# Gate projections of blocks two to four by seven half-size products, with prepared weight combinations, gating in token halves, and a new stage order

## The chip, the cores and the metric

The kernel runs on one core of one Trainium2 chip. The metric is the device time in microseconds (us) of one execution. A core has a matrix engine (TensorE, PE, with a separate row for its weight loads, PEld), three engines for element-wise work (VectorE or DVE, ScalarE or ACT, GpSimd or POOL), and a queue engine (SyncE, SP) that issues nearly all DMAs of this kernel. Each engine works through its own list of instructions in order.

## The reference

One decoder layer on x of 2048 tokens by 1024 columns, in float32:

```python
n = _rms_norm(h, attn_norm_w[l])
proj = jnp.einsum('bsd,dc->bsc', n, w_in[l])
(gq, gk, gv, gg, ga, gb, rq, rk, rv, rg) = jnp.split(proj, split_idx, axis=-1)
o_gdn = _gated_deltanet(gq, gk, gv, gg, ga, gb, ...)
o_ret = _retention(rq, rk, rv, rg)
mix = jnp.concatenate([o_gdn, o_ret], axis=-1)
h = h + jnp.einsum('bsm,md->bsd', mix, w_out[l])
n2 = _rms_norm(h, mlp_norm_w[l])
h = h + _conv_glu_mlp(n2, w_up[l], mlp_conv_w[l], w_down[l])
return _rms_norm(h, final_norm_w)
```

Both head groups have 4 heads of 128 columns. The delta-rule group (gdn) carries a 128x128 state per head through the sequence; retention does the same with a fixed decay. The gates gg and rg, 512 columns each, are 1024 of the projection's columns. They enter only at the end of the mixer, where the normalized output of each head is multiplied by silu of its gate.

## The kernel before

Every float32 matmul is made of three passes with operands split in two parts, a high part (ACT copies it into the reduced type) and a low part (DVE subtracts the high part from the source): high by high, high by low, low by high. `mm3` (lines 108 to 113) issues the three passes; their matmuls are recorded as L111, L112, L113. A token-major projection, `tokmajor` (lines 375 to 387), issues the same three passes as L383, L384, L385.

The kernel has three stages. The mixers work through the sequence in four blocks of 512 tokens. MLP up (`mlp_up`) and MLP down (`mlp_down`) then each work on all 2048 tokens.

Large products are done by a scheme with seven half-size products in place of eight (the Strassen-Winograd form): both operands are cut into four quarters, sums and differences of quarters are formed, seven products are computed, and their results are added. Before the change the output projection of each block (items W1 to W7), MLP up and MLP down are computed so. The input projections, the gates among them, are plain.

A mixer block consists of named items: `pro` (load x, norms), `k0`, `q0`, `kq`, `v0` (retention projections, token-major), `a0` to `a3` (gdn projections of one head, channel-major, tile name chm), `b0`, `b1` (`gdn_base`: triangular inverse of 32x32 blocks, a long serial series on POOL, L603 and L605), `g0`, `g1` (`gdn_lvls` and four steps `gdn_rec` of the recurrence, then `gdn_fin`, for a pair of heads), `h0` to `h3` (retention heads), `p0`, `p1` (the gate projections, `gates`, 512 columns each: half gdn, half retention), `G0`, `G1` (`gated`: factor times gate, 32 PE transposes a block, tiles mix and mxt), `W1` to `W7` (output products), `N` (norm and transposes for the MLP, nps).

A recurrence step is a series over engines: PE (ks, L679), DVE (L682), PE (wps, L690), DVE (L694), PE (sps, L698), DVE (state, L700). `gdn_fin` makes the norm factor of all four steps with a power function on POOL (L716), and `gated` multiplies with it.

The string `ORDER` (lines 41 to 46) lists the items of all four blocks in one sequence, the first character being the block. The program is traced in this order; a scheduler then fixes the order of each engine's instructions before the run, with the traced order as priority, so that later items may fill time in which earlier ones wait for their inputs. Buffer counts per tile name (`BUFS`, `NWV` and others) limit how far ahead this goes.

Weights: `load_chunk` (lines 262 to 286) loads a projection's weights. In block one it reads them raw, splits them on ACT and DVE (L279, L280) and writes the split form to DRAM (wd); later blocks read it back (L273, tiles wc, 512 KB each). The gate weights are 16 such tiles a block. The weights of the output products are made by `load_v` (lines 154 to 193): in block one it loads quarters of the weight matrix for each product (wvr), forms the combination on POOL (L177), splits it (L197, L198), and writes it to DRAM (L192); later blocks read it back (L162, tiles wv, 5 buffers). `load_v` also serves MLP down (tiles vr, vt, v), where it forms every product's combinations anew.

`with tc.issue_after(ins)` queues what it encloses behind `ins` on the same engine's list: issue order only, no wait for the end of `ins`. Before the change the first weights and the x of MLP up are placed so behind one x load of block four's first output product (`FENCE`, lines 1079 to 1084).

Of the kernel before, what the change touches and what calls it, by code (L numbers as in the profile page):

```python
# [8 lines left out]
F32 = mybir.dt.float32  # L9
# [17 lines left out]
NWV = 5  # L27
FX = 1
NU = 4
NPB = 8  # L30
# [10 lines left out]
ORDER = ("0pro 0k0 0v0 0dec 0a0 0q0 0a1 0a2 0h0 0b0 0h1 0a3 0b1 0g0 0kq 0g1 0h2 0p1 1pro 0p0 1k0 0G0 0h3 "  # L41
# [37 lines left out]
def hybrid_block(ctx, tc, x, xT, w_kq, w_v, w_g, w_rk, w_r0, w_r, w_o, w_u, w_d, cols, rows, fnr, masks, rot, out):  # L79
# [28 lines left out]
    def mm3(ps, pairs, first=True, chk=False):  # L108
        n = len(pairs)
        for i, (ah, al, bh, bl) in enumerate(pairs):  # L110
# [11 lines left out]
           for q in range(2) for i in range(1, 8)}  # L122

    items = mixers(ctx, tc, base, o, marks, drp, mm3, gamma, mhalf, n1w, n2w, gcw, gv127, epsr, gnw, n2d, hd,
                   x, xT, w_kq, w_v, w_g, w_rk, w_r0, w_r, w_o, rows, masks, rot)
# [9 lines left out]
    for i, it in enumerate(seq):  # L135
# [3 lines left out]
        if it[0] is not None:  # L139
            it[2](loaded.pop(i))  # L140
# [7 lines left out]
    mlp_down(tc, marks, mm3, sfa, mhalf, hd, aud, w_d, fnr, out)  # L148
# [5 lines left out]
def load_v(tc, pool, w, i, k, tags, kept=None, drp=None):  # L154
# [5 lines left out]
    if kept is not None and (i, k) in kept:  # L160
        v = mk("v", F32R)
        nc.sync.dma_start(v.bitcast(F32), kept[i, k])  # L162
        return v
# [25 lines left out]
    v = split_v(nc, mk("v", F32R), src)  # L189
    if kept is not None:  # L190
        kept[i, k] = drp.tile([P, 2, TB], F32, name=f"wo{i}_{k}", tag=f"wo{i}_{k}", bufs=1)
        nc.sync.dma_start(kept[i, k], v.bitcast(F32))  # L192
    return v
# [9 lines left out]
def mixers(ctx, tc, base, base_used, marks, drp, mm3, gamma, mhalf, n1w, n2w, gcw, gv127, epsr, gnw, n2d, hd,  # L203
# [52 lines left out]


    WQ = 264
    cache = {}
    uses = {}  # L260

    def load_chunk(key, src):
# [1025 lines left out]
```

## Time and profile before

| what | value |
|---|---|
| median of 3 runs | 2495.26 us (2492.26 to 2498.91) |
| span of the profiled execution | 2495.3 us |
| granted TensorE clock, mean | 0.993 |
| PE busy | 2414.8 us (97%), 12476 matmuls |
| DVE, ACT, POOL busy | 1621.8, 1001.3, 579.7 us |
| DMA | 609.64 MB, 244 GB/s mean |

The profiled execution's own time is its span, from the first to the last instruction. In the groups of instructions a row gives line, engine, operation, output and input tiles, shape and count, then busy time, the mean of one in ns, and the idle time of the engine just before. Matmuls are pipelined, so that the means of neighbouring matmuls overlap. In the stretches the columns after the length are the busy time of PE, PEld, DVE, ACT and POOL, the granted clock, the share of time the DMA engines were busy, and GB/s.

### The profile page before, as it was taken

To read this page: it belongs to the slowest core of one execution; us is meant where nothing else is said; L and a number is where in the kernel's file an instruction comes from. 1 tells how busy PE (TensorE), PEld (TensorE's weight loads), DVE (VectorE), ACT (ScalarE), POOL (GpSimd) and SP (SyncE) were. 2 spreads that over 40 slices of the span, in tenths; PEclk is the share of its full clock that TensorE was granted. 3 is DMA by queue.
4 is the path that set the end of the run, shared out by engine and by line. 5 is a ranking of instruction groups with operands and counts; after the bars stand their busy time and mean duration, and the time that the engine had idled before them with its cause. 6 is when DMAs were issued, how large, how long until landed. Compare 5 with 4: busy or idle time off the path is not lost.

```text
span 2495.3 us, 35737 instructions
## 1 busy us (share of the span) xinstructions
PE 2414.8 (97%) x12476; PEld 2022.8 (81%) x12476; DVE 1621.8 (65%) x3199; ACT 1001.3 (40%) x2152; POOL 579.7 (23%) x891
## 2 busy tenths in 40 slices
PE   8999899999999999998899999999999999999998
PEld 7877787887888878887688888888888888888877
DVE  5845776435652673536889888896565567555795
ACT  6544544434342552425464344442222225332332
POOL 1354146521046205140011000010000001521180
PEclk9999999999999999999999999999999999999999
DMA  8756498863865646643889887867676868764794
GB/s 326 253 183 243 166 328 301 283 224 117 300 214 162 213 178 228 232 168 136 335 338 347 303 300 292 297 257 277 225 261 234 288 235 279 222 218 142 238 295 135
DMA packets 285748, 609.64 MB, mean 244 GB/s; under 512 B 40896, under 2 KB 120960, under 8 KB 285568
## 3 DMA queue, kind: packets, MB, share of 16 engines
q1 hardware_dynamic: 268992, 593.06, 67.7%
q10 hardware_dynamic: 16576, 14.30, 1.8%
q8 instruction: 98, 1.61, 0.3%
q14 instruction: 82, 0.67, 0.1%
HBM read 410.56 MB, written 196.71 MB: 243 GB/s over the span
## 4 chain that ended last, share of the span: by engine, by line
PE 76%; POOL 8%; DMA 6%; DVE 5%; issue 3%; ACT 2%; SPq 0%; ACTq 0%; POOLq 0%; DVEq 0%
PE p L111 10%; PE p L112 10%; PE p L113 10%; PE d L113 5%; PE d L111 4%; PE d L112 4%; PE tok L383 4%; PE tok L385 4%; PE tok L384 4%; POOL pers L605 3%; POOL pers L603 3%; PE chm L111 2%; PE chm L112 2%; PE chm L113 2%; PE wo L111 1%
## 5 line engine op out<-in xcount | busy, mean ns | idle before, releaser
L112 PE MATMUL p<-x,wu 128*128 128x512 f32 x1176 | 458.6, 390 | 4.2 <-DVE x L929 4.2
L111 PE MATMUL p<-x,wu 128*128 128x512 f32 x1176 | 454.4, 391 | 5.2 <-ACT x L928 3.8
L113 PE MATMUL p<-x,wu 128*128 128x512 f32 x1176 | 450.9, 389 | 0.0
L383 PE MATMUL tok<-wc,n 128*128 128x512 f32 (+2 forms) x768 | 275.4, 363 | 10.1 <-ACT n L371 8.4
L384 PE MATMUL tok<-wc,n 128*128 128x512 f32 (+2 forms) x768 | 276.7, 361 | 0.0
L385 PE MATMUL tok<-wc,n 128*128 128x512 f32 (+2 forms) x768 | 275.2, 362 | 0.0
L111 PEld LDWEIGHTS p<-x,wu 128*128 128x128 f32 x1176 | 220.8, 188 | 54.7 <-ACT x L928 6.5
L112 PEld LDWEIGHTS p<-x,wu 128*128 128x128 f32 x1176 | 220.8, 188 | 51.7 <-DVE x L929 6.4
L113 PEld LDWEIGHTS p<-x,wu 128*128 128x128 f32 x1176 | 220.9, 188 | 45.6
L1049 DVE SCALAR_TENSOR_TENSOR acc<-uc,base,acc 128x1022 f32<-128x1022 f32 (+1 forms) x176 | 221.1, 1278 | 39.8 <-ACT acc L1046 38.3
L1007 DVE TENSOR_TENSOR uc<-p,uc 128x512 f32<-128x512 f32 x224 | 153.0, 685 | 134.7 <-PE p L113 134.1
L177 POOL TENSOR_TENSOR vt<-vr 128x512 f32<-128x512 f32 x44 | 71.7, 1635 | 613.0 <-DMA vr<-in_w_d 439.3
L111 PE MATMUL d<-v,uu 128*128 128x512 f32 x448 | 174.4, 389 | 0.0
L113 PE MATMUL d<-v,uu 128*128 128x512 f32 x448 | 174.4, 389 | 0.0
L112 PE MATMUL d<-v,uu 128*128 128x512 f32 x448 | 174.4, 389 | 0.0
L383 PEld LDWEIGHTS tok<-wc,n 128*128 128x128 f32 x768 | 146.5, 191 | 29.7 <-ACT n L371 8.4
L384 PEld LDWEIGHTS tok<-wc,n 128*128 128x128 f32 x768 | 146.3, 191 | 19.3
L385 PEld LDWEIGHTS tok<-wc,n 128*128 128x128 f32 x768 | 145.1, 190 | 19.3
L111 PE MATMUL chm<-n,wc 128*128 128x512 f32 x384 | 152.3, 397 | 0.0
L113 PE MATMUL chm<-n,wc 128*128 128x512 f32 x384 | 152.3, 397 | 0.0
L112 PE MATMUL chm<-n,wc 128*128 128x512 f32 x384 | 152.1, 396 | 0.0
L1054 POOL COPY base<-uc 128x2 f32<-128x2 f32 x44 | 40.9, 929 | 451.1 <-DVE uc L1007 451.1
(250 smaller groups left out, 4857.6 us busy)
## 6 DMA issues: line engine op xcount, KB each, us to landing
wu<-wu SPq DMA_DIRECT2D x308, 512.0 KB, 6.0
wc<-wd SPq DMA_DIRECT2D x166, 512.0 KB, 5.1
wv<-wo SPq DMA_DIRECT2D x84, 512.0 KB, 5.4
wd<-wc SPq DMA_DIRECT2D x60, 512.0 KB, 4.2
ur<-au SPq DMA_DIRECT2D x56, 512.0 KB, 5.4
wur<-in_w_u SPq DMA_DIRECT2D x44, 512.0 KB, 5.9
au<-st SPq DMA_DIRECT2D x88, 256.0 KB, 4.8
vr<-in_w_d SPq DMA_DIRECT2D x44, 512.0 KB, 6.1
```

The lines of the kernel that those rows point to most:

```text
L111: PE.matmul(ps, ah, bh, start=(first and i == 0), stop=False, skip_group_check=chk)
L112: PE.matmul(ps, ah, bl, start=False, stop=False, skip_group_check=chk)
L113: PE.matmul(ps, al, bh, start=False, stop=(i == n - 1), skip_group_check=chk)
L177: POOL.tensor_tensor(tt[:, j], a, b_, op=ALU.subtract)
L383: PE.matmul(ps, ah, wh, start=(k == 0), stop=False)
L384: PE.matmul(ps, ah, wl, start=False, stop=False)
L385: PE.matmul(ps, al_, wh, start=False, stop=(k == KT - 1))
L603: POOL.tensor_tensor(tm[:, :, :n], Nb[:, j:j + 1, j + 1:].to_broadcast([P, 8, n]), X[:, :, j:j + 1].to_broadcast([P, 8, n]), op=ALU.mult)
L605: POOL.tensor_tensor(X[:, :, j + 1:], X[:, :, j + 1:], tm[:, :, :n], op=ALU.add)
L1007: add = lambda o, ps, a: DVE.tensor_tensor(o, ps, a, op=ALU.add)
L1049: DVE.scalar_tensor_tensor(acc[:, t:], u[:, :T2 - t], w, acc[:, t:], op0=ALU.mult, op1=ALU.add)
L1054: POOL.tensor_copy(mhalo[:, ci], u[:, T2 - 2:])
```

## The change

Gates: block one keeps the two plain projections (items p0, p1). In blocks two to four they are replaced by seven products B1 to B7 over tokens (2 x 256), input columns (2 x 512) and gate columns (2 x 512, array w_i). The item `s` (`combs`) loads the block's x once more and forms four combinations; `product` splits them when it first needs them, and adds the results up. Gates are now held as four tiles of 128 tokens by 1024 columns (C, Cb).

Weight combinations: the items Q0 to Q3 (output weights) and P0 to P3 (gate weights), one per K-tile, load four quarters once, form all combinations with four subtractions on POOL, split all seven and write them to DRAM (`prep_v`). Every product then reads its tiles back, in block one too (`kept_v`), through the same 5 buffers wv. These loads are `chained`: each is queued behind the previous one on SP, and behind the last load of the projection before. The gate weights' split form is no longer written by `load_chunk`.

Gating: `gated` works on tokens 0 to 255 (items G0a, G1a) and 256 to 511 (G0b, G1b) apart; the recurrence steps are single items (r00 to r13), and `gdn_fin` is called after every second step for half the tokens.

Others: MLP up's first weights and each quarter of its x are placed behind loads of block four's last output product (`FW`, `F0` to `F3`). In MLP down the combination made for product 6 is written to DRAM (t2d), and product 4 is made from it with one subtraction in place of three. Buffer counts and `ORDER` are new.

```diff
-FX = 1
-NU = 4
-NPB = 8
+FW = -3
+F0 = -4
+F1 = -3
+F2 = -2
+F3 = -1
+NU = 5
+NPB = 7
...
-BUFS = {"n1": 8, "ykq": 5, "kv": 4, "NT": 5, "AT": 6, "o": 2, "n2s": 11, "xk": 2, "og": 1, "co": 6, "Cw": 4,
-        "wx": 1, "wsq": 3, "wvr": 3, "wvt": 8, "ca": 8, "mix": 6, "D": 8, "rk": 5, "rq": 4, "rv": 8, "Ar": 1,
-        "Nb": 6, "rot": 1, "rrow": 7}
+BUFS = {"n1": 8, "ykq": 5, "kv": 5, "NT": 8, "AT": 8, "o": 2, "n2s": 11, "xk": 2, "og": 9, "co": 6, 
+        "Cw": 6, "wx": 1, "wsq": 1, "pr": 4, "pt": 7, "pv": 2, "ca": 4, "D": 8, "rk": 3, "rq": 9, "rv": 5, 
+        "Ar": 2, "xs": 6, "sx": 2, "Cb": 14, "Nb": 1, "rot": 1, "rrow": 1}
...
+ORDER = ("0pro 0k0 0dec 0v0 0a0 0q0 0a1 0a2 0h0 0h1 0a3 0b0 0Q0 0L0 0r00 0b1 0L1 0r01 0r02 0r03 0r10 0r11 "
+         "0r12 0r13 0kq 0Q1 0h3 0p1 1pro 0p0 0Q3 0h2 1k0 0Q2 0G1a 0G1b 0G0a 1v0 1dec 0W1 0G0b 0W2 0P3 1a0 1q0 "
+         "1a1 0W6 0W7 1h1 0W5 0W3 0W4 1a2 1h0 0P0 1b0 0N 1kq 1L0 1r00 0P2 1s 1r01 0P1 1a3 1B1 1B2 1B6 1r02 "
+         "1r03 1h2 1B7 1G0a 1b1 1L1 1r10 1r11 2pro 1B5 1B3 1h3 1B4 2k0 1r12 1r13 2v0 1G1a 1G1b 1G0b 2dec 1W1 "
+         "1W2 2a0 1W6 2a1 2a3 2b0 2a2 1W7 2b1 1W5 2q0 2L0 1W4 2h1 2r00 1W3 2r01 2h0 2r02 2r03 2L1 2r10 3pro "
+         "2r11 2s 2B1 2B2 2B6 2r12 2G0a 2r13 2B7 1N 2kq 2B5 2h2 2h3 2B4 2G0b 2B3 3k0 3dec 2G1a 2G1b 3a1 3a0 "
+         "2W1 3b0 2W2 2W6 2W7 3v0 3a2 3q0 3h1 3h0 2W5 3a3 3B1 3L0 3r00 3b1 3r01 3kq 3r02 3s 3B2 3L1 2W3 3h2 "
+         "3G0a 3r10 2W4 3r03 3B6 3r11 3r12 3r13 3B7 3B5 3B4 3B3 2N 3h3 3G1a 3W1 3G1b 3W2 3G0b 3W6 3W7 3W5 3W3 "
+         "3W4 3N")
...
+def chained(tc, marks, dst, src):
+    with tc.issue_after(marks["sp"].ins) if "sp" in marks else nullcontext():
+        marks["sp"] = tc.nc.sync.dma_start(dst, src)
+    marks.setdefault("vl", []).append(marks["sp"])
+def prep_v(tc, pool, marks, w, k, nm, kept, drp, caps):
...
+    for d, a, b_ in ((t1, q[1], q[0]), (t3, q[3], q[1]), (t2, q[3], t1), (t4, q[2], t2)):
+        POOL.tensor_tensor(d, a, b_, op=ALU.subtract)
+    for i, src in ((1, q[0]), (2, q[2]), (3, q[3]), (5, t1), (7, t3), (6, t2), (4, t4)):
+        v = split_v(nc, unit(pool, "pv", [P, 2, TB], F32R, bufs=caps[2]), src)
+        kept[i, k] = drp.tile([P, 2, TB], F32, name=f"{nm}{i}_{k}", tag=f"{nm}{i}_{k}", bufs=1)
+        nc.sync.dma_start(kept[i, k], v.bitcast(F32))
...
-                if keep:
+                if keep and key[0] != "g":
...
+        def combs(_):
...
+                for i, d, op, a, b_ in ((5, a22, ALU.add, a21, a22), (7, a21, ALU.subtract, a11, a21),
+                                        (6, a11, ALU.subtract, a22, a11), (3, a12, ALU.subtract, a12, a11)):
+                    DVE.tensor_tensor(d, a, b_, op=op)
+                    st["sr"][i, j] = d
...
+        def product(i):
+            def f(_):
+                ws = [kept_v(wic, i, k) for k in range(4)]
+                if i in (5, 6, 7, 3) and (i, 0) not in st["sx"]:
+                    for j in range(2):
+                        x_ = st["sx"][i, j] = al("sx", [P, 2, 2, TB // 2], F32R)
+                        split_v(nc, x_, st["sr"][i, j])
...
+                if i in (1, 5):
+                    st["ps"] = [bank("pi") for m in range(2)]
+                pss = st["ps"] if i in (1, 2, 3, 5) else [bank("pi") for m in range(2)]
+                for m in range(2):
+                    ps = pss[m]
+                    mm3(ps, [xop(i, k, m) + (ws[k][:, 0], ws[k][:, 1]) for k in range(4)],
+                        first=i not in (2, 3), chk=i in (2, 3))
...
+        def use_b(t, half_, src, dst):
+            ACT.activation(dst, src, AF.Silu, scale=st["r"][:, t:t + 1])
...
-        def gated(g):
+        def gated(g, hf):
...
+                        for c in range(2 * hf, 2 * hf + 2):
...
+                if c % 2:
+                    gdn_fin(hs, c // 2)
...
-                vs = [load_v(tc, ap_, w_o, i, k, {"vr": ("wvr", BUFS["wvr"]), "vt": ("wvt", BUFS["wvt"]), "v": ("wv", NWV)},
-                             wvc, drp) for k in range(NH)]
+                vs = [kept_v(wvc, i, k) for k in range(NH)]
+                if b == NB - 1:
+                    marks.setdefault("wo", []).extend(marks["vl"][-NH:])
...
-    FENCE = [("x", NB - 1, 0, 0), ("x", NB - 1, 1, 0), ("x", NB - 1, 2, 0), ("x", NB - 1, 3, 0)]
+    fence = [marks["wo"][j].ins for j in (FW, F0, F1, F2, F3)]
-    with tc.issue_after(marks[FENCE[FX]].ins):
+    with tc.issue_after(fence[0]):
         nxt = load_w(*gs[0])
-        xc = prep_x(0)
+    xc = prep_x(0, fence[1:])
...
+    if t2d is not None and i == 4:
+        r = mk("vr")
+        nc.sync.dma_start(r[:, 0], t2d[k])
+        nc.sync.dma_start(r[:, 1], w[k, :, 2 * TB:3 * TB])
+        tt = mk("vt")
+        POOL.tensor_tensor(tt[:, 0], r[:, 1], r[:, 0], op=ALU.subtract)
+        return split_v(nc, mk("v", F32R), tt[:, 0])
```

More of the change, by code (lines that the diff above doesn't have):

```diff
@@ L375, in tokmajor, with gates, f, evac @@
+        def gates(g):
+            def f(w):
+                if "C" not in st:
+                    st["C"] = [al("Cb", [P, D]) for t in range(NT)]
+                def evac(t, ps):
+                    use_b(t, 0, ps, st["C"][t][:, g * TB:(g + 1) * TB])
+                tokmajor(w, 512, evac)
+            return f
+        def use_b(t, half_, src, dst):
+            ACT.activation(dst, src, AF.Silu, scale=st["r"][:, t:t + 1])
         def tokmajor(w, ncol, evac):
```

209 lines of the change are left out of this document (138 added, 71 removed), and 5 rows, old and new, of the table ORDER.

## The prediction

> **What bounds the kernel now.** I read the page first (engine totals, the slices, the chain), then the busy time by stage, then PE's own list of waits, then the stretches where PE stands.
>
> ```profile
> span 2495.3 us, 35737 instructions
> PE 2414.8 (97%) x12476; PEld 2022.8 (81%) x12476; DVE 1621.8 (65%) x3199; ACT 1001.3 (40%) x2152; POOL 579.7 (23%) x891
> PE   8999899999999999998899999999999999999998
> PEclk9999999999999999999999999999999999999999
> GB/s 326 253 183 243 166 328 301 283 224 117 300 214 162 213 178 228 232 168 136 335 338 347 303 300 292 297 257 277 225 261 234 288 235 279 222 218 142 238 295 135
> PE 76%; POOL 8%; DMA 6%; DVE 5%; issue 3%; ACT 2%; SPq 0%; ACTq 0%; POOLq 0%; DVEq 0%
> ```
>
> PE is busy for 97% of the span, has three quarters of the chain, and its clock is near full: this is a PE-bound kernel. The 80 us in which PE does nothing decide how far a saving gets. Busy time in three stretches, mixers (0 to 1302 us, with the first MLP products mixed into their end), MLP up, MLP down; columns are the stretch, its length, busy time of PE, PEld, DVE, ACT, POOL, clock, DMA share and GB/s:
>
> ```profile
> 0.00:1302.00 1302.00, 1231.07 (x7260) 1044.19 (x7261) 766.87 (x2054) 585.15 (x1537) 407.90 (x761) 0.99 0.66 234
> 1302.00:2063.00 761.00, 760.99 (x3357) 629.94 (x3357) 577.41 (x812) 265.25 (x365) 34.55 (x37) 1.00 0.77 277
> 2063.00:2495.30 432.30, 422.77 (x1862) 348.69 (x1860) 277.53 (x334) 150.93 (x251) 137.22 (x93) 1.00 0.69 217
> 1750.00:2000.00 250.00, 250.00 (x1104) 207.04 (x1104) 144.90 (x211) 60.63 (x70) 0.00 (x0) 1.00 0.70 247
> ```
>
> The up stage has no idle PE at all. 1302.00 − 1231.07 = 70.9 us of the idle time is in the mixers, 9.5 us in the down stage, 7 of those behind the last matmul. The fourth row gives the unit of account: 250.00 us / 1104 = 0.2264 us from one 128x512 matmul to the next in a full stream. The mean of one instruction in the groups (390 to 397 ns) overlaps its neighbours and is no price.
>
> **The dense work that goes.** In blocks two to four the gates were two projections of 8 K-tiles x 4 token tiles x 3 passes x 2 = 192 matmuls of 128x512; now they are 7 products x 2 x 4 K-tiles x 3 = 168, same shape. 72 fewer in all: 72 x 0.2264 = 16.3 us. The transposes of the gating stay at 32 a block. In a PE-bound stage this is a full saving unless its place is taken by idle time.
>
> **What the seven products add elsewhere.** These groups are the nearest rows; columns are line, engine, operation, tiles, shape and count, busy time and mean of one, idle before:
>
> ```profile
> L198 DVE TENSOR_TENSOR wv<-wvt,wv 128x512 fp32r<-128x512 f32 x16 | 12.7, 793 | 30.0 <-ACT wv L197 30.0
> L198 DVE TENSOR_TENSOR wv<-wvr,wv 128x512 fp32r<-128x512 f32 x12 | 8.1, 693 | 1.0 <-ACT wv L197 1.0
> L197 ACT ACTIVATE wv<-wvt 128x512 fp32r<-128x512 f32 x16 | 10.1, 630 | 33.6 <-POOL wvt L177 30.4 <-DMA wvr<-in_w_o 3.0
> L177 POOL TENSOR_TENSOR wvt<-wvr 128x512 f32<-128x512 f32 x16 | 22.2, 1390 | 39.1 <-PE chm L113 13.2 <-DMA wvr<-in_w_o 9.6 <-DVE pers L337 5.8
> L845 DVE TENSOR_TENSOR Cw<-wo,Cw 128x512 f32<-128x512 f32 x56 | 37.1, 684 | 22.4 <-PE wo L113 22.3
> L371 ACT ACTIVATE n<-xk,base 128x512 fp32r<-128x512 f32 x32 | 22.2, 720 | 11.9 <-PE tok L385 9.4 <-DMA xk<-in_xT 2.4
> L1128 DVE TENSOR_TENSOR uu<-ur,uu 128x1024 fp32r<-128x1024 f32 x56 | 79.8, 1427 | 64.2 <-ACT uu L1127 43.4 <-PE d L113 16.4 <-DMA ur<-au 2.8
> ```
>
> Once, the four P stages: 28 splits, 28 x 0.63 = 17.6 us on ACT and 28 x 0.75 = 21 on DVE (between the two L198 rows), and 16 subtractions on POOL, 16 x 1.39 = 22. The four Q stages move the splits of the output weights and need 16 subtractions in place of 28 (16.7 us less). Per later block: 8 scaled copies (8 x 0.72 = 5.8, ACT), 8 combinations (8 x 0.68 = 5.4, DVE), 8 splits of 1024 columns (8 x 1.43 = 11.4 on DVE, some 8 on ACT), 10 additions of the results (10 x 0.68 = 6.8, DVE). That is 24 us of DVE a block, 93 with the P stages, on 766.87 us in 1302: from 59% to about 68%. ACT goes from 45% to about 50%. Neither comes near PE; I price it at nothing. The cover is the dense PE stream, and it is missing only in the bare recurrences at block ends; if one addition of 0.68 us stood ahead of each hop over DVE there (3 a step, 4 steps, 4 ends: 48), it would cost up to 33 us, the other end.
>
> The Trainium skill, "SBUF — State Buffer", section "Who interferes with whom", says that a DVE instruction with two SBUF inputs is locked out while a GpSimd instruction reads SBUF. The rows lean that way: 793 against 693 ns with POOL's tiles about. By the rule each of the 16 new POOL subtractions could hold DVE once, at most 22 us, in block one, where DVE has some 40% idle: the sum stays.
>
> **Weights: twice the bytes per matmul.** A gate matmul stream took 8 tiles of 512 KB in 96 x 0.2264 = 21.7 us, 193 GB/s. A half-size product takes 4 tiles (2.10 MB) in 24 x 0.2264 = 5.43 us, 386 GB/s, through five slots shared with the output products. In all the DMA grows by about 37 MB (later blocks 3 x 8.4, P stages 4.2 in and 14.7 out, output weights 4.2 more, cached gate weights 8.4 less, down stage 2.9 less). Rows: issues with their median time to landing, two stretches of time, PE's waits.
>
> ```profile
> wc<-wd SPq DMA_DIRECT2D x166, 512.0 KB, 5.1
> wv<-wo SPq DMA_DIRECT2D x84, 512.0 KB, 5.4
> 300.00:400.00 100.00, 98.68 (x497) 83.17 (x496) 78.22 (x165) 45.35 (x111) 33.94 (x33) 1.00 0.88 309
> 1182.00:1250.00 68.00, 58.78 (x234) 44.24 (x235) 56.35 (x94) 31.20 (x54) 1.73 (x2) 0.97 0.90 342
> PE wo L111 <- ACT wv L197: 4.3, 1, 4.3
> PE wps L690 <- DVE kv L682: 5.9, 11, 1.0
> PE sps L698 <- DVE pers L694: 5.9, 11, 0.8
> PE d L113 <- DVE u L1128: 2.4, 2, 1.8
> SPq L162 <- PE wo L113: 21.2, 16, 3.8
> ```
>
> 386 GB/s is above anything in the page (347 in the best slice). Alone, a product would be paced by its loads: at 342 GB/s it takes 6.13 us, 0.70 more; at 309, 6.79, 1.36 more. For 21 products that is 15 to 28 us. Against it: the 84 loads wv<-wo feed products of exactly this form in blocks two to four, and no row of PE's waits names a DMA; other blocks' projections run in between. I take the end at nothing, since that is the nearest row, and keep 28 as the other. What queues behind a load that waits for its slot (last row) is everything later on SP, the next projection's weights first, as the new chaining fixes SP's order.
>
> The Trainium skill, "DMA: Bandwidth & Descriptors", section "Where 436 GB/s comes from", puts the limit of HBM to SBUF at about 358 GB/s a core, which speaks against this change: 2.10 MB would take 5.86 us, 0.43 too long, and 21 bare products 9 us (estimate from that page), so 2471 in place of the sum below. This trace reaches 347, so it does not contradict it.
>
> **Output weights in own stages.** Block one's output products were fed by the POOL, ACT and DVE work above while PE waited; PE's row names 4.3 us for the split. With the Q stages a block earlier in the order that wait goes: 4.3 us (bounds 0 and 8.6, as the loads are now written and read back).
>
> **Gating in halves.** At each block's end the recurrence runs bare. Two of the four stretches and the sum of all four; pieces of one step of the recurrence; the start of the output products of block four and, in the row of tok, the start of the last projection's last matmul (1125.3); and two rows for the next two parts, the first request of the MLP's x and a stretch of the down stage:
>
> ```profile
> 598.00:619.00 21.00, 15.05 (x107) 12.59 (x105) 12.72 (x48) 11.47 (x46) 2.64 (x2) 1.00 0.28 96
> 1127.00:1168.00 41.00, 32.74 (x256) 28.95 (x253) 26.05 (x95) 23.68 (x82) 5.30 (x4) 1.00 0.24 85
> sum 116.90, PE 86.44 PEld 75.22 DVE 79.83 ACT 68.14 POOL 18.24; mean PE 21.61 PEld 18.80 DVE 19.96 ACT 17.03 POOL 4.56
> 1153.77 0.74 PE L690 MATMUL wps<-kv,AT 128*128 128x128 f32 x4 [0.44 <-DVE kv L682]
> 1156.59 1.20 PE L679 MATMUL ks<-pers,ykq 128*128 128x128 f32 x8 [0.44 <-DVE pers L700]
> 1168.24 0.50 PE L111 MATMUL wo<-wv,wu 128*128 128x512 f32 x1 [1.39 <-ACT wu L872]
> L385 PE MATMUL tok<-wc,n x768: 277/389/628, 10.3 to 1125.3; 128*128 128x512 f32 x128, 128*128 128x264 f32 x32, 128*128 128x256 f32 x32
> 1181.23 7.46 DMA xr<-n2d
> 2362.00:2422.00 60.00, 58.20 (x257) 47.86 (x257) 53.20 (x50) 19.29 (x34) 49.73 (x32) 1.00 0.99 317
> ```
>
> 116.90 − 86.44 = 30.5 us idle (the other two stretches are 257 to 293 and 884 to 903). The first two products, 48 x 0.2264 = 10.9 us, need only tokens 0 to 255; until now they waited for all four steps and the gating (1168.24 in block four). Now they are free two steps earlier and fill the second half of each end. About half of the idle time lies there, and the chain of gating, copy and split eats part: I take a third, 10.2 us (bounds 0 and 30.5). The factors are computed twice as often, in half the width; POOL's power function stands on that path either way.
>
> **Start of MLP up.** x was requested during the first output products of block four (1181 us); now weights and x stand behind the last product's loads. In 1182 to 1250 PE already loses 68.00 − 58.78 = 9.2 us while DMA runs at 342 GB/s. Later x leaves the output products their bandwidth, but 5 MB then land at 342 GB/s in 15 us after them, with only the last product's 5.4 us to cover: gain 9, loss 9. I take 0.
>
> **Down stage.** One of its products takes a saved intermediate, so 22 of its 33 subtractions on POOL go. There PE's row shows 2.4 us of waiting for DVE (u L1128). In 2362 to 2422, while the last product's operands were made, DVE is busy for 53.20 of 60 us, POOL for 49.73, and DMA's share is 0.99; with the lighter operands that wait goes, 2.4 (bounds 0 and 2.4).
>
> **Sum.** The profiled execution took 2495.3, the same as the median 2495.26 of the three runs, so no correction. 2495.3 − 16.3 − 10.2 − 4.3 − 2.4 = 2462.
>
> **Rivals.**
> *More goes than the sum has.* All dense work can be placed anew: half of the 70.9 us idle in the mixers goes, with 16.3 and 2.4: 2495.3 − 35.5 − 16.3 − 2.4 = 2441. For it: the steps of the recurrence are now single items between dense products. Against: waits of 0.44 us inside a step are latency and remain where no matmul is ready.
> *The gain is eaten.* The gate matmuls were themselves the filling of the recurrences; 16.3 us less filling leaves 16.3 us more bare chain, and halves gain nothing: 2495.3 − 2.4 = 2493, no change. For it: the bare ends stand there because filling ran out (tok ends at 1125, output starts at 1168). Against: most of blocks two and three is full.
> *Slower.* SP's fixed order and the five slots pace the 21 products at 309 GB/s, bare: 2495.3 − 16.3 + 28.4 = 2507. It decides from the point at which more than 60% of the products lack other work beside them (16.3 of 28.4). For it: 386 GB/s wanted, and several products stand next to each other in the order. Against: the list of PE's waits without a DMA.
>
> **How the numbers follow.** Forecast 0.53 (its own range 2448 to 2484, from the bounds of gating and weights), more 0.16, eaten 0.14, slower 0.17. The range 2436 to 2508 reaches to both outer cases. This kernel's three runs lie within 0.3%, so a difference under that cannot be told from none, 7.5 us: faster is the forecast, "more" and 0.01 of "eaten", 0.70; same 0.13; slower 0.17.
>
> **What would show it.** PE instructions down by 72, to 12404; products of the gates at 0.226 us a matmul. If a DMA row heads PE's waits, or SP's waits for the slots of wv grow far beyond 21 us with PE idle between products, the slower case holds. Idle PE in the mixers: 55 or so by the sum, 35 by "more", 85 by "eaten". In the down stage the row of waits for DVE u should be gone. If up starts with more than 10 us of idle PE, the fences cost what I set at nothing.

## The result and the profile after

The changed kernel is slower: 2519.07 us (median of four, 2515.36 to 2527.24) against 2496.68 for the kernel before, measured beside it; ratio 1.0098, 95% interval 1.0076 to 1.0119. Forecast were 2462, range 2436 to 2508. Differences below are taken from ratios times 2495, since the median of the kernel before differs by up to 4 us from one comparison to the next; a ratio's interval reaches 2 to 8 us to each side, and the difference of two changed kernels is known to some 4 to 9 us.

The page of the kernel after, its totals, DMA and the chain that ended last:

```profile
span 2513.5 us, 36031 instructions
PE 2412.1 (96%) x12404; PEld 2016.1 (80%) x12404; DVE 1688.0 (67%) x3329; ACT 1048.3 (42%) x2206; POOL 595.5 (24%) x881
...
DMA packets 296550, 646.63 MB, mean 257 GB/s; under 512 B 42096, under 2 KB 122160, under 8 KB 296368
...
PE 58%; DVE 8%; DMA 7%; POOL 4%; issue 2%; ACT 2%; SPq 0%; ACTq 0%; POOLq 0%; DVEq 0%
```

The 72 matmuls are gone (12404) and DMA grew by 37 MB, both as forecast. But PE's busy time fell by 2.7 us and not by 16.3, and PE's share of the chain fell from 76% to 58%. (The two profiled executions are 18.2 us apart, 2513.5 against 2495.3, less than the medians; two of the three other executions of the kernel after had a mean clock of 0.984, where the profiled one had 0.988.) Now the stretch from the start to the 500th matmul of MLP up, the same work in both; columns as in the prediction (stretch, length, busy PE, PEld, DVE, ACT, POOL, clock, DMA share, GB/s). The kernel before, with some stretches of it:

```profile
0.00:1341.00 1341.00, 1270.07 (x7432) 1076.48 (x7433) 799.52 (x2098) 602.35 (x1562) 412.23 (x765) 0.99 0.67 238
...
300.00:550.00 250.00, 241.01 (x1309) 202.79 (x1308) 141.59 (x331) 104.54 (x272) 117.13 (x192) 0.99 0.79 278
...
700.00:800.00 100.00, 99.72 (x633) 85.26 (x632) 39.14 (x116) 34.19 (x105) 64.82 (x133) 1.00 0.54 180
800.00:900.00 100.00, 94.83 (x690) 83.84 (x689) 61.68 (x217) 46.06 (x120) 20.31 (x38) 1.00 0.56 196
...
1100.00:1200.00 100.00, 86.09 (x597) 71.59 (x596) 62.57 (x169) 50.13 (x138) 5.30 (x4) 0.98 0.46 164
1200.00:1300.00 100.00, 95.02 (x413) 75.21 (x412) 85.12 (x129) 50.03 (x75) 9.17 (x11) 1.00 0.87 326
```

The kernel after:

```profile
0.00:1359.70 1359.70, 1267.50 (x7360) 1069.60 (x7361) 888.30 (x2232) 650.46 (x1621) 466.69 (x777) 0.98 0.73 264
...
300.00:550.00 250.00, 224.20 (x1278) 188.97 (x1277) 172.03 (x430) 123.45 (x330) 90.32 (x129) 0.98 0.80 289
...
700.00:800.00 100.00, 89.20 (x577) 75.85 (x577) 61.15 (x155) 41.97 (x113) 73.57 (x140) 0.95 0.72 245
...
1200.00:1300.00 100.00, 89.77 (x368) 69.82 (x367) 80.56 (x127) 53.26 (x86) 15.24 (x8) 0.91 0.88 334
...
1359.70:2092.80 733.10, 730.94 (x3221) 604.21 (x3220) 551.00 (x778) 252.34 (x343) 31.57 (x33) 1.00 0.75 272
```

Idle PE in this stretch went from 1341.0 − 1270.1 = 70.9 us to 92.2, and the clock fell. The three places where PE loses most are the preparation of the weights (300 to 550), 700 to 800, and the start of MLP up (1200 to 1300). The last row shows 2.2 us of idle time in MLP up, which had none.

From the starts of the matmuls in both traces the stretch can be split further: matmuls of each width times their undisturbed spacing (work), time between a matmul's end and the next one's start (idle), time by which matmuls under half clock are longer (half clock), and what is left, between small matmuls (rest). From the first matmul on, us; e10, e13 and e14 are experiments described below:

| kernel | length | work | idle | half clock | rest |
|---|---|---|---|---|---|
| before | 1332.6 | 1193.8 | 62.6 | 12.0 | 64.3 |
| after | 1349.7 | 1177.5 | 82.2 | 21.9 | 68.1 |
| e10: new order, plain gates | 1337.5 | 1193.8 | 66.8 | 14.8 | 62.2 |
| e13: e10 less 72 matmuls | 1342.0 | 1177.5 | 79.0 | 21.0 | 64.5 |
| e14: before less 72 matmuls | 1324.9 | 1177.5 | 60.1 | 23.5 | 63.8 |

The 16.3 us did leave the work. Idle time took 19.6 back, the clock 9.9, the rest 3.8. What PE waits for in the kernel after (us in total, times, longest), and what SP waits for:

```profile
PE tok L519 <- ACT n L417: 10.0, 1, 10.0
PE wo L118 <- DMA wv<-wo: 8.4, 4, 2.5
PE pi L118 <- DMA wv<-wi: 8.1, 8, 2.5
```

```profile
SPq L164 <- PE wo L120: 57.1, 30, 8.9
SPq L164 <- PE pi L120: 49.9, 34, 7.6
```

Weight loads now stand second and third among PE's waits, 16.5 us, where no DMA was named, and SP waits 107 us for slots of wv where it was 21. The prediction called that the sign of its "slower" rival, and the experiments test it first.

### The profile page after: what moved, and what is told of

It is laid out like the page before. It is cut to its first block, busy times and chain, and to the rows that moved or that the text cites. A ratio compares the mean times of both kernels' runs of the same rounds, so it can differ in the third digit from the quotient of the medians.

```text
span 2513.5 us, 36031 instructions
## 1 busy us (share of the span) xinstructions
PE 2412.1 (96%) x12404; PEld 2016.1 (80%) x12404; DVE 1688.0 (67%) x3329; ACT 1048.3 (42%) x2206; POOL 595.5 (24%) x881
## 4 chain that ended last, share of the span: by engine, by line
PE 58%; DVE 8%; DMA 7%; POOL 4%; issue 2%; ACT 2%; SPq 0%; ACTq 0%; POOLq 0%; DVEq 0%
PE p L118 9%; PE p L119 9%; PE p L120 9%; PE d L119 5%; PE d L120 5%; PE d L118 5%; POOL pers L731 2%; DMA wv<-wi 2%; POOL pers L729 2%; DMA wur<-in_w_u 1%; DVE acc L1181 1%; PE pi L118 1%; DMA wu<-wu 1%; PE tok L519 1%; PE pi L119 1%
## 5 line engine op out<-in xcount | busy, mean ns | idle before, releaser
L519 PE MATMUL tok<-wc,n 128*128 128x512 f32 (+2 forms) x576 | 200.0, 353 | 14.8 <-ACT n L417 10.0
L520 PE MATMUL tok<-wc,n 128*128 128x512 f32 (+2 forms) x576 | 202.0, 351 | 0.0
L521 PE MATMUL tok<-wc,n 128*128 128x512 f32 (+2 forms) x576 | 199.4, 350 | 0.0
L212 POOL TENSOR_TENSOR vt<-vr 128x512 f32<-128x512 f32 x33 | 52.2, 1590 | 517.4 <-DMA vr<-in_w_d 446.2
L729 POOL TENSOR_TENSOR pers<-Nb,pers 128x248 f32<-128x248 f32 (+30 forms) x248 | 124.2, 501 | 66.2 <-DMA Nb<-z 49.7
L731 POOL TENSOR_TENSOR pers<-pers 128x248 f32<-128x248 f32 (+30 forms) x248 | 132.7, 535 | 17.3
L519 PEld LDWEIGHTS tok<-wc,n 128*128 128x128 f32 x576 | 110.9, 193 | 28.7 <-ACT n L417 10.0
```

Source lines behind the costliest of these rows:

```text
L212: POOL.tensor_tensor(tt[:, j], a, b_, op=ALU.subtract)
L519: PE.matmul(ps, ah, wh, start=(k == 0), stop=False)
L520: PE.matmul(ps, ah, wl, start=False, stop=False)
L521: PE.matmul(ps, al_, wh, start=False, stop=(k == KT - 1))
L729: POOL.tensor_tensor(tm[:, :, :n], Nb[:, j:j + 1, j + 1:].to_broadcast([P, 8, n]), X[:, :, j:j + 1].to_broadcast([P, 8, n]), op=ALU.mult)
L731: POOL.tensor_tensor(X[:, :, j + 1:], X[:, :, j + 1:], tm[:, :, :n], op=ALU.add)
```

## The experiments

### Are the weight loads the bound? (e1, e2)

e1, half the loads of the gate products:

```diff
-                ws = [kept_v(wic, i, k) for k in range(4)]
+                ws = [kept_v(wic, i, k) for k in range(2)] * 2
```

> The changed kernel, but each of the 21 gate products loads only two of its four weight tiles (the tiles of K-tiles 0 and 1 stand in for 2 and 3 too, so the gates of blocks two to four are other numbers); matmuls, splits, writes and stage order stay. Against before, the changed kernel's profile has 16.3 us less dense work up to the 500th MLP matmul, but 20 us more idle PE and 10 us more lost at half clock; 18 us of PE's waits name weight tiles wv. Theory 'loads': the gate products' tiles come too late, PE waits, and the clock drops after each wait; with half the tiles those waits (8 us named for pi, part of 8 for wo) and part of the clock loss go: 2500 to 2508. Rival 'order': the loss is from the new stage order and the added element-wise work; then 2515 to 2522 as with the change.

e2, eight slots:

```diff
-NWV = 5
+NWV = 8
```

> The changed kernel with 8 buffers for the tiles wv in place of 5, nothing else. Theory 'loads' in its form 'slots': a load waits for the release of one of five tiles (SP waits 57 and 50 us for matmuls of wo and pi); with eight it starts three tiles earlier, the DMA waits of PE (18.7 us) mostly go: 2498 to 2508. In its form 'bandwidth', or if SP's fixed order is what holds the loads: little, 2512 to 2522. Rival 'order': 2515 to 2522.

e1: 2525.25 us, ratio 1.0128 (1.0097 to 1.0159). e2: 2526.31, 1.0129 (1.0113 to 1.0145). Neither is faster than the change (1.0098). PE's waits for these weights did get shorter, from 16.5 us to 12.2 in e1 and 9.8 in e2:

```profile
PE wo L118 <- DMA wv<-wo: 7.6, 5, 2.2
PE pi L118 <- DMA wv<-wi: 4.6, 4, 1.5
```

```profile
PE wo L118 <- DMA wv<-wo: 5.3, 2, 4.1
PE pi L118 <- DMA wv<-wi: 4.5, 6, 1.7
```

Half the bytes of the gate products and three more slots buy no time, so neither bytes nor slots pace the kernel, although the waits have that look: a list of waits tells what came last, not what the time would be without it. The third part of that rival, SP's fixed order, was loosened for the output weights only (e11 below).

### Which part of the change costs it? (e3, e4, e10)

e3 keeps all of the change but the seven products: plain gates p0 and p1 in every block, without P, s and B. e10 is e3 with the early request of MLP up (below). e4 is the kernel before with the change's MLP down alone:

```diff
+    if t2d is not None and i == 4:
...
+        nc.sync.dma_start(r[:, 0], t2d[k])
+        nc.sync.dma_start(r[:, 1], w[k, :, 2 * TB:3 * TB])
...
+        POOL.tensor_tensor(tt[:, 0], r[:, 1], r[:, 0], op=ALU.subtract)
```

> The changed kernel with the gates of blocks two to four as plain projections again (two per block, at the places of the first and the fourth or fifth product; no P stages, no combinations of x), all else as changed: Q stages, halves, single recurrence steps, fences, down stage. Theory 'loads': the dense work comes back (16.3 us), but with it go the late tiles, the P stages and their traffic: 2490 to 2500, at or under before. Rival 'order': what was lost stays and 16 us come on top: 2525 to 2538.

> The kernel before with the down-stage part of the change alone (the saved combination, one subtraction in place of three). In the changed kernel's profile the down stage is 3.3 us shorter from its first idle time on (416.6 to 413.3 us after the last up matmul). If that is this part's doing: 2492 to 2495 against 2496.7, and the 2.4 us of waiting for DVE u gone. If it came with the rest: no change.

e3: 2507.13, ratio 1.0053 (1.0034 to 1.0071). With the matmuls of before put back it is 11 us faster than the change (4 to 18). e4: 2492.08, 0.9988 (0.9977 to 0.9999), 3 us faster than before; of the kernels here that leave no work out it is the only one faster than before.

### Does the late request of MLP up cost? (e6, e7, e10)

e6, in the kernel before, later; e7, in the change, earlier:

```diff
-FX = 1
+FX = 3
```

```diff
-FW = -3
-F0 = -4
-F1 = -3
-F2 = -2
-F3 = -1
+FW = -11
+F0 = -12
+F1 = -11
+F2 = -10
+F3 = -9
```

> The kernel before with one number changed: MLP up's first weights and x are queued behind the last x load of block four's fifth output product (FX = 3) in place of the first product's. Theory 'late up': what the changed kernel loses between 1200 and 1300 us (10 us of idle PE and a clock of 0.91, against 5 us and 1.00) comes from requesting x so late; then this costs 5 to 12 us: 2500 to 2507. Rival: the output products get their weights sooner for it, and it is even: 2492 to 2497.

> The changed kernel with its five marks eight loads earlier: MLP up's weights and x behind the loads of the fifth output product of block four in place of the last one's. Theory 'late up': 5 to 10 us go, 2509 to 2514. Rival: x then takes the bandwidth of the last two output products, even: 2516 to 2522.

> Plain gates as in the third run and MLP up requested eight loads earlier as in the seventh. If the two causes add up: 2507 less 8 to 14 us, 2493 to 2499, level with before. If the early request only helps where seven products load weights: 2503 to 2508.

e6: 2508.78 against 2494.27, ratio 1.0065 (1.0050 to 1.0080): one number, 16 us (12 to 20). The stretch in e6, and its waits over the whole run:

```profile
1200.00:1300.00 100.00, 82.00 (x321) 62.19 (x321) 81.48 (x127) 55.23 (x89) 8.63 (x9) 0.85 0.86 316
```

```profile
PE p L111 <- ACT x L928: 8.9, 6, 3.6
```

PE waits for the split of an x that came late, 18 of 100 us are idle, and the clock falls to 0.85 on top. The traces also show what the early request was good for. In the kernel before, MLP up's first matmul starts at 1182.6 us and the last output product's at 1248.2, so that the two fill each other's gaps; in e6 the output products end at 1204.3 and up starts at 1210.4. In the change they hardly overlap (1219.3 and 1222.5), in e7 they do again (1210.0 and 1250.1).

e7: 2511.32, 1.0072 (1.0057 to 1.0088), 6.5 us faster than the change; e10: 2500.52, 1.0029 (1.0017 to 1.0041), 6 faster than e3. Both differences are about as large as their uncertainty (6.6 and 5.5); the clear evidence is e6. In e7 the same stretch has its clock back, though as much idle time as the change (10.2 us):

```profile
1200.00:1300.00 100.00, 89.80 (x386) 70.96 (x386) 85.54 (x134) 51.62 (x85) 5.50 (x9) 0.97 0.82 308
```

Taken at its middle value, that is a quarter of the loss. In the two profiles it doesn't all arrive: half clock lasts 6.8 us in place of 17.1 from 1180 to 1310, but 51.2 in place of 23.9 from 300 to 1180.

### The side work of the seven products (e5, e9, e15)

e5 keeps one preparation stage of four (its K-tile serves all four); e9 leaves out the x combinations:

```diff
-                ws = [kept_v(wic, i, k) for k in range(4)]
+                ws = [kept_v(wic, i, 3) for k in range(4)]
```

```diff
-            if i in (1, 2, 4):
-                n1 = st["n1"][kt + (0 if i == 1 else 4)]
+            if i:
+                n1 = st["n1"][kt + (0 if i in (1, 7) else 4)]
...
-                if i in (5, 6, 7, 3) and (i, 0) not in st["sx"]:
+                if False:
```

In e5 the items 0P0 to 0P2 leave the order, in e9 the items s. e15 is e5 with the early request of e7.

> The changed kernel with one P stage in place of four: the tiles of K-tile 3 stand in for the other three (the gates of blocks two to four are other numbers); the products load as many tiles as before. Left out: 21 splits (13 us of ACT, 15 of DVE), 12 subtractions on POOL (17 us), 3.1 MB read and 11 MB written, all between 340 and 530 us, where the changed kernel has 18.8 us of idle PE in 400 to 600 against 4.6 with plain gates. Theory 'crowding': the P stages hold up the short chains of blocks one and two on DVE, ACT and SP: 8 to 14 us go, 2505 to 2512. Rival 'products': what PE loses there is the products' own structure (their slots, their splits and additions, their place between recurrence steps): 2515 to 2523.

> The changed kernel without the combinations of x: products 5, 6, 7 and 3 take the plain normed x in their place (the gates of blocks two to four are other numbers). Left out per later block: 2 MB of x read again, 8 scaled copies, 8 combinations, 8 splits of 1024 columns (about 17 us of DVE and 14 of ACT); matmuls, weight loads, additions and order stay. Theory 'crowding': what the seven products lose beyond the P stages is DVE, ACT and SP work in front of the short chains: 6 to 12 us go, 2507 to 2513. Rival 'products': their place, slots and additions lose it: 2515 to 2523.

> The changed kernel with the edits of e5 and e7 together: one preparation stage P in place of four (the products use its K-tile for all four, so that the gates are not the reference's) and the early request of MLP up. If the two losses are apart, as the theory has it, 2519 - 8 - 8 = 2503. If both were one loss that was pushed along, 2510 or more.

e5: 2511.22, ratio 1.0068 (1.0051 to 1.0085), 7.5 us faster than the change. Its stretch of preparation and a later one:

```profile
300.00:550.00 250.00, 238.59 (x1364) 203.20 (x1365) 160.20 (x427) 118.75 (x317) 74.94 (x125) 0.98 0.71 256
...
700.00:800.00 100.00, 84.18 (x560) 71.89 (x559) 55.86 (x149) 39.99 (x113) 68.89 (x137) 0.97 0.67 227
```

PE gets 14.4 us of this stretch back (224.20 to 238.59), and the run half of that, with an uncertainty of 6.8; 700 to 800 gives 5.0 away again (89.20 to 84.18). e9: 2515.30, 1.0086 (1.0071 to 1.0101), 3 us, less than the intervals can tell. e15: 2508.10, 1.0059 (1.0044 to 1.0074): with both edits 9.7 us in place of 14. That is what a loss that moves would look like, but 9.7 is known to 6.5 us, so that the two may as well add up.

### Can 16.3 us of matmuls be saved here at all? (e13, e14)

The gates of blocks two to four without their last K-tile have the change's matmul count and none of its side work (`tokmajor` gets the number of K-tiles as a parameter; loads stay):

```diff
-                tokmajor(w, 512, evac)
+                tokmajor(w, 512, evac, KT if b == 0 else KT - 1)
```

> The kernel of e10 (plain gates in all blocks, early request of MLP up), in which the gate projections of blocks two to four use seven of their eight K-tiles: one K-tile of each is left out of the sums, so that the gates are not the reference's. It has the matmul count of the changed kernel, 12404, with none of the products' additions, combinations and preparation. Theory 'products' own work' (the 16.3 us of dense matmuls can be saved, and the seven products lose them by what they bring with them): 2500.5 - 16 = 2484. Rival 'filling' (the gate matmuls were the filling of the recurrences, so that idle time takes the place of what goes): 2500, within 4 us.

> The kernel before with the same edit: gate projections of blocks two to four without their eighth K-tile, so that the gates are not the reference's, and nothing else changed. Theory 'products' own work': 2495 - 16 = 2479. Rival 'filling': 2491 or more, as the bare ends of the blocks grow by what goes.

e13 (from e10): 2504.71, ratio 1.0045 (1.0030 to 1.0060). 72 matmuls less, and not faster than e10 (1.0029) or e16 (1.0025); if anything 4 us slower. e14 (from before): 2488.44, 0.9985 (0.9973 to 0.9997): 4 us arrive of 16.3 (1 to 7; 7.7 up to this point in the two profiles of the table). "Products' own work" is out in both, and "filling" is the nearer. In the table above the new order turns the missing work mostly into idle time (e13 − e10: idle +12.2, half clock +6.2), the old order into half clock (e14 − before: +11.5, with no more idle time). The stretch of e14:

```profile
0.00:1333.20 1333.20, 1264.85 (x7360) 1071.21 (x7361) 802.06 (x2102) 606.39 (x1567) 409.95 (x765) 0.98 0.67 240
```

72 matmuls of 0.226 us are gone, and PE's busy time fell by 5.2 us only: the others took longer. Why, the clock shows. Two windows of 3.4 us near 870 us (the clock is granted window by window, see the last section), e14 first, then the kernel before:

```profile
869.80:873.20 3.40, 1.80 (x13) 1.45 (x13) 3.40 (x11) 1.03 (x3) 0.00 (x0) 1.00 0.00 0
873.20:876.60 3.40, 2.95 (x12) 2.38 (x11) 1.10 (x6) 1.65 (x7) 0.00 (x0) 0.50 0.00 0
```

```profile
869.80:873.20 3.40, 3.40 (x23) 3.04 (x22) 1.74 (x6) 1.38 (x5) 0.00 (x0) 1.00 0.03 8
```

What PE does there, in e14 and in the kernel before:

```profile
868.04 1.05 PE L679 MATMUL ks<-pers,ykq 128*128 128x128 f32 x8
869.54 0.75 PE L690 MATMUL wps<-kv,AT 128*128 128x128 f32 x4 [0.44 <-DVE kv L682]
871.01 0.68 PE L698 MATMUL sps<-pers,kv 128*128 128x128 f32 x4 [0.72 <-DVE pers L694]
873.01 1.94 PE L679 MATMUL ks<-pers,ykq 128*128 128x128 f32 x8 [0.88 <-DVE pers L700]
```

```profile
867.83 1.05 PE L679 MATMUL ks<-pers,ykq 128*128 128x128 f32 x8
868.63 0.48 PE L113 MATMUL chm<-n,wc 128*128 128x512 f32 x1
```

Before, 512-wide matmuls of a projection (chm) stand between the steps of the recurrence and fill this window. They are no gate matmuls: with less gate work ahead of them, in e14 all 936 chm matmuls up to here have run by 868 us, where 58 were left before, and the recurrence stands bare. PE is then busy for 1.80 of 3.40 us, a little over half, and the next window runs at half clock, in which the same eight matmuls of ks take 1.94 us in place of 1.05. So the work that is missing need not show where it was taken out.

### The new order itself (e8, e11, e12, e16, e17, e18)

With plain gates and the early request, e10 still stands 7 us above before, and its worst stretch after the first block is 700 to 800 (the two rows behind it serve below); then SP's longest wait there:

```profile
700.00:800.00 100.00, 88.87 (x604) 75.95 (x603) 47.66 (x129) 30.17 (x80) 60.25 (x130) 0.97 0.60 202
800.00:900.00 100.00, 100.00 (x670) 88.65 (x669) 49.89 (x182) 41.55 (x105) 16.11 (x29) 1.00 0.58 210
...
1100.00:1200.00 100.00, 90.06 (x575) 75.98 (x575) 55.89 (x165) 46.03 (x124) 11.30 (x17) 0.98 0.53 199
```

```profile
SPq L156 <- POOL pers L723: 12.5, 1, 12.5
```

A load of output weights stands for 12.5 us behind POOL's serial inverse, with all later loads behind it; PE then waits 7.5 us for loaded output weights in this stretch. Three edits tried to take that away: output weights' loads not chained (e11, from e7), six buffers for the inverse as before (e16, from e10), the store of the inverse issued by POOL (e17 from e10, e18 from e7):

```diff
-                vs = [kept_v(wvc, i, k) for k in range(NH)]
+                vs = [kept_w(i, k) for k in range(NH)]
```

```diff
-        "Ar": 2, "xs": 6, "sx": 2, "Cb": 14, "Nb": 1, "rot": 1, "rrow": 1}
+        "Ar": 2, "xs": 6, "sx": 2, "Cb": 14, "Nb": 6, "rot": 1, "rrow": 1}
```

```diff
-                nc.sync.dma_start(z2.rearrange("h c k (g a) i -> (h c k g) (a i)", g=4), X.rearrange("p c i -> p (c i)"))
+                nc.gpsimd.dma_start(z2.rearrange("h c k (g a) i -> (h c k g) (a i)", g=4), X.rearrange("p c i -> p (c i)"))
```

(kept_w is kept_v with a plain load in place of the chained one.)

> The changed kernel with MLP up requested eight loads earlier, and the loads of the output products' tiles no longer chained to SP's order (those of the gate products stay so). In the changed kernel's profile SP stands for 12.1 us before a load of wv (it waits for POOL L731, whose tiles held that memory), and PE then waits 8.4 us for DMA wv<-wo in 700 to 800. Theory 'SP order': free of the chain such a load is placed where it doesn't hold the others: 2500 to 2506. Rival: with the early request alone it was 2511, and it stays there: 2508 to 2514.

> The kernel of e10 with six buffers for the tile Nb of POOL's serial inverse, as before the change, in place of one. Theory 'memory': the load of output weights that stands for 13 us behind POOL near 730 us, and the idle time of PE after it, come from memory that the inverse still holds; with more buffers the wait of SP for POOL's tile pers goes from 700 to 800 us and the time falls by 5 to 10 us, to 2491 to 2495. Rival 'order': the loads stand behind the inverse for the order of the series itself; then nothing changes, 2500.

> The kernel of e10 (plain gates, new order, early request of MLP up), with one edit: the store of the finished triangular inverse (z from pers) is issued by POOL's own queue and not by SP. Theory 'head of the line': SP stands 12.5 us behind POOL near 715 us because the store of the inverse is on its list ahead of loads that are wanted, and what PE waits there for output weights (7.5 us in that stretch, and some half clock after it) follows from it; then SP's wait for POOL's pers goes, PE's busy time in 700 to 800 us rises from 88.9 towards 99, and the time falls by 6 to 11 us, to 2490 to 2494. Rival 'gone elsewhere': the order of the items sets it and the loss moves; 2498 to 2503.

> The kernel of e7 (the change with the early request of MLP up), with the same edit. Theory 'head of the line': 2511 - 6 to 11 = 2500 to 2505. Rival 'gone elsewhere': 2508 to 2514.

e11: 2524.82, ratio 1.0121 (1.0104 to 1.0138), 12 us slower than e7: in this order the chaining of these loads is worth something. e16: 2500.61, 1.0025 (1.0014 to 1.0037), no change. e17: 2496.75, 1.0017 (1.0006 to 1.0027). e18: 2518.93, 1.0106 (1.0091 to 1.0121), 8.5 us slower than e7 by the same edit. SP's wait stays, in e16 first, then in e17:

```profile
SPq L156 <- POOL pers L723: 12.5, 1, 12.5
```

```profile
SPq L156 <- POOL pers L723: 12.0, 1, 12.0
```

So neither the number of the inverse's buffers nor its store holds the load up. In the traces of e3, e10, e16 and e17 alike the load is issued 0.03 us after the end of the inverse's last instruction that reads the tile Nb (L721; 727.50 and 727.53 us in e10), before the last L723 begins. Why a load of wv waits for that instruction stays open, and so does how much of the 7 us it makes.

Two more runs on the order: e8, a control, exchanges two neighbours in the order of before. e12 has the seven products in blocks three and four only, with the P stages behind block two's output products, where the trace of e10 looked dense.

```diff
-2kq 2h2 2p0 2G0
+2kq 2p0 2h2 2G0
```

> A control: the kernel before with two neighbouring items of the stage order exchanged in block three (a retention head and a gate projection, which do not depend on each other). No work is added, removed or moved far. If the place of a stall depends on the fixed order in detail, this alone moves the time by several us either way: 2485 to 2510. If only the amounts of work count: within 2 us of 2495.

> Seven products in blocks three and four alone, block two's gates plain; the four P stages moved behind block two's output products, where POOL is busy for 6 of 100 us and DMA for half of the time; MLP up requested eight loads earlier. 48 matmuls less, 10.9 us. Theory 'crowding' (the P stages cost what they do because they lie beside the work of blocks one and two): 2484 to 2492, under before. Rival 'products' (each block of seven products loses more than its 5.4 us wherever it stands): 2497 to 2506.

e8: 2494.32, ratio 1.0002 (0.9993 to 1.0011): that detail carries nothing in the order of before. e12: 2583.17, 1.0359 (1.0343 to 1.0375). Its worst stretch, PE's longest wait over the run, and two of SP's waits from 690 to 800 us:

```profile
700.00:800.00 100.00, 51.16 (x333) 41.74 (x331) 39.38 (x89) 18.03 (x49) 58.10 (x110) 0.68 0.43 144
```

```profile
PE wo L110 <- DMA wv<-wo: 29.8, 8, 12.7
```

```profile
SPq L175 <- DVE pv L223: 18.4, 6, 10.3
SPq L725 <- POOL pers L723: 15.2, 1, 15.2
```

DMA moves 144 GB/s, so bandwidth is free; SP stands behind the stores of the preparation (pv) and of the inverse, with the loads of wv behind them on its list. The preparation was expected to cost less in this place and did not; whether a place without urgent loads behind it would be cheap was not tried.

## Why the prediction was wrong

The steps from before to after, by runs: to e10 +7.2 us (predicted −16.9: gating, output weights, down), e10 to e7, which puts the seven products in, +10.7 (predicted −16.3), e7 to the change +6.5 (predicted 0). They add up to the 24.4 measured (0.0098 x 2495), as they must. Of the 10.7, 4.0 come as the matmuls go (e13 against e10) and 6.7 with what the products bring along (e7 against e13, the same number of matmuls), each known to some 5 us.

**The dense work, −16.3: wrong in kind.** The step said "a full saving unless its place is taken by idle time". The count was right, the spacing too, but the place was taken: e13 gains nothing by the same matmuls and e14 4 us. This is the rival "the gain is eaten", with a second taker that it did not have: the clock. Idle PE of the mixers came out at 92 us, near the 85 that the prediction had named for that rival. The kernel was called PE-bound because PE was busy for 97% of the span (95% of the mixers); but matmuls that are ready also fill the waits of the recurrence, and when 72 of them are gone, PE waits or runs at half clock. That the recurrence sets the time there is how I read the rows of e14; no run shortens the recurrence itself to prove it, and what e14 would take at full clock isn't known.

**The side work, 0: wrong.** The step priced it at nothing under a dense PE stream. All that the products bring costs 6.7 us by e7 against e13. The P stages alone measure 3.2 (e15 against e7, inside the intervals) and 7.5 (e5 against the change, just outside). They run where block one's own work is in flight, and the 300 to 550 rows show PE short of work, not DVE full (172 of 250 us). The rule that the prediction weighed for these instructions (the Trainium skill, "SBUF — State Buffer", "Who interferes with whom") is not seen to matter; DVE's half of the splits, minimum, median and maximum in ns, in the kernel before (two groups) and in the one after:

```profile
L198 DVE TENSOR_TENSOR wv<-wvt,wv x16: 674/692/1570, 314.1 to 452.9; 128x512 fp32r<-128x512 f32 x16
L198 DVE TENSOR_TENSOR wv<-wvr,wv x12: 679/683/794, 18.6 to 387.9; 128x512 fp32r<-128x512 f32 x12
L231 DVE TENSOR_TENSOR pv<-pr,pv x24: 676/693/1810, 107.4 to 512.9; 128x512 fp32r<-128x512 f32 x24
```

The medians are the same (692 and 683 before, 693 after); a few are held up in both. The 793 and 693 ns that the prediction compared were means, which such a few can raise.

**Weights, 0 of 28: right for bytes and slots, against the look of the trace.** e1 and e2 show it. The rival "slower" came nearest in sign and size (2507), but by luck: its price was 28 us for pacing by loads, and easing the loads gained nothing. The 358 GB/s that the Trainium skill gives ("DMA: Bandwidth & Descriptors", "Where 436 GB/s comes from") is no ceiling on this one core either; e1 passes it over 100 us (last column):

```profile
1200.00:1300.00 100.00, 87.37 (x350) 65.00 (x349) 75.68 (x124) 52.17 (x86) 15.06 (x7) 0.93 0.97 372
```

**Start of MLP up, 0: wrong, 6.5 us here and 16 in the order of before.** The step set a gain of 9 against a loss of 9. The loss is real (e6); the gain, bandwidth for the output products, did not show. What it left out is that up's first matmuls had been running beside the output products. Its own sign, more than 10 us of idle PE where up starts, was just there, 10.2 us in 1200 to 1300 (5.0 before), but e7 has 10.2 too; the difference is in the clock. The 2.2 us inside up lie later, 1.7 of them at 1675 us.

**Gating in halves, −10.2, and output weights, −4.3: neither arrived.** There are hints of both mechanisms. In e10, PE is busy for 100.00 us in 800 to 900 and 90.06 in 1100 to 1200, two stretches in which the kernel before has its bare ends, against 94.83 and 86.09 there; these are stretches of time, and the two kernels do not do the same work in them. The PE wait for the split of wv is gone. But the new order loses 10.9 us at 700 to 800, PE waits for loaded output weights in the split's place (11.5 us in e10, 8.4 in the change), and idle time as a whole rose, from 62.6 to 66.8 us in the table. With down's 3 us in, the sum to e10 is a loss of 7.2. No run takes the halves or the output weights' own stages out alone, so which of them failed isn't known.

**Down stage, −2.4: right.** Its wait for DVE u is gone and e4 gains 3 us (0.3 to 5.7).

What stays open: why the load at 715 us waits for POOL, which part of the new order costs the 7 us, and how the rest of the loss splits between the filling and the side work. The scheduler lays out each engine's list anew for every edit, so that each difference of a few us can hold some of that.

## What to carry to other kernels

A stage whose engine is busy for 95% can still give back only a part of the work that is taken out: before pricing removed work at full value, drop the same amount of work and time it, as e14 does with a few lines. Price idle time of PE with what the clock adds. Where operands are prepared in stages of their own, look at what stands behind their transfers on the same queue, and keep the next stage's first loads early enough that its first matmuls run beside the last ones of this stage.

## What the hardware showed

**The clock is granted by a grid of 3.413 us, and it doesn't take an empty window to lose it.** In all twenty traces the records of half clock last 3.413 us or a multiple of it, but for the one that the end of the program cuts off, and within a trace they start on one grid. Three grid windows of the kernel after:

```profile
728.10:731.50 3.40, 3.40 (x21) 2.98 (x20) 3.40 (x6) 2.03 (x9) 3.01 (x6) 1.00 0.81 241
731.50:734.90 3.40, 1.20 (x6) 0.68 (x4) 3.03 (x11) 3.20 (x15) 2.91 (x7) 1.00 0.60 220
734.90:738.30 3.40, 3.17 (x9) 2.62 (x10) 0.23 (x2) 0.00 (x0) 2.79 (x9) 0.51 0.00 0
```

Counted over the grid windows of the twenty traces that were at full clock and less than 90% busy: of 148 windows in which PE was busy for under 40%, all were followed by half clock; from 40 to 45%, 35 of 38; from 45 to 65%, 46 of 259; above, 1 of 664. By these counts a wait of 2 us inside one window costs up to 1.7 us more in the next (an estimate: half of 3.413). The Trainium skill, "TensorE: Matmul & The Clock Gate", "What's actually happening", gives the period (about 3.4 us) and half speed after an idle window; the period agrees, but here a window does it that is far from empty, with PE busy for 40% and mostly even for 45%. The records of half clock add up to 36 us in the profile of before and 60 in that of after; 5 to 6 us of each lie behind the last matmul.

**One edit, two answers.** Moving one store to POOL's queue changed e10 by −3 us (inside the intervals) and e7 by +8.5. An effect of a few us in these mixers need not transfer from one order to another.
